# Experts' weights as plain fp32 on two 64-column halves of the PE array, unsplit, with contiguous stationary operands and 16 raw weight buffers

## The chip, the core and the metric

The kernel runs on one core of one Trainium2 chip. The metric is the device time of one execution in microseconds; of several executions the median counts. One execution was also recorded by the hardware profiler, and all rows below come from that record. The engines are called PE (matrix products; PEld is its load of the stationary operand), DVE (vector), ACT (scalar functions), POOL (GpSimd) and SP (the queue that starts most transfers).

## The reference, cut to what matters

Two model blocks follow each other on 256 tokens of width 1024. The change touches only the end of the second one, a mixture of 32 experts in four groups. Every token goes to two experts of one group; an expert is a gated unit of width 512.

```
def _hier_moe(h, rt_g, rt_g_b, rt_e, rt_e_b, ex_gate, ex_up, ex_down):
...
    top_val, top_idx = lax.top_k(le_grp, TOP_K_IN_GROUP)
    wts = jax.nn.softmax(top_val, axis=-1) * p_top
    e_flat = (grp[:, None] * E_PER_GROUP + top_idx.astype(jnp.int32)).reshape(-1)
...
    def expert_block(args):
        idx, w, e = args
        xb = tok_pad[idx]
        hb = jax.nn.silu(xb @ ex_gate[e]) * (xb @ ex_up[e])
        return (hb @ ex_down[e]) * w[:, None]
```

All is float32. The weights of one expert are three matrices of 2 MB each.

## The kernel before, in words

The program is written with a scheduler that orders the instructions of each engine by priority and readiness and places the semaphores. Products that need more than one pass of PE's fast fp32r format are made from an exact pair of parts: a high part (ACT casts the fp32 tile to fp32r, line 141) and a lower part (DVE subtracts it from the fp32 tile, line 142).

The last stage is `Block2.moe` (line 2265). `route` (line 1906) finds each token's experts, normalises and modulates the tokens (lines 1947 to 1950) and splits them into the parts `tok` (`xh`, `xl`). The pairs of token and expert are laid out in slots of 64 rows, one or more for each expert. 29 slots are always worked on (`SURE`); code for up to 39 stands behind a branch. The experts of the first `FIXED` slots are known without routing, so their weights can be fetched early (`fetch`, line 2095).

`slots` (line 2225) runs a software pipeline over the slots. For slot j:

- `gather` (line 2125), for slot 0 alone and then for four slots at once, multiplies one-hot masks with the tokens' parts: 32 products with the token columns as stationary operand, taken with a stride of 8 elements. It gives X, with 64 columns of high and 64 of low parts for each of 8 row blocks.
- `slot_up` (line 2148) fetches gate and up weights in four pieces of 1 MB. Each is cast and subtracted into parts (`split_w`, line 161). For each row block there is one product of X (128 stationary columns: high and low together) with the weights' high part, and one of X's 64 high columns with the weights' lower part. They collect in one bank of PSUM, whose lower 64 rows hold what the low parts of X give.
- `slot_hidden` (line 2169) transposes by a product with `both`, which adds the two row halves, applies the gate, and splits the result into H. The stationary operand G is read with a stride of four elements.
- `slot_down` (line 2187) does the same as `slot_up` with H and two pieces of the down weights, for the slot before; the result is scaled and split into Y.
- `slot_add` (line 2210) adds Y to the tokens' rows through a one-hot mask that POOL builds, for the slot before that.

Raw weights lie in 8 tiles of 8 KB a partition (`raws(8)`, line 2345), their parts in 6 pairs of half tiles (`parts(3)`). Transfers of weights are issued by SP in order; each waits until its raw tile is free, which is when ACT and DVE have read it. In the routing, splits of the first pieces are held back behind the masks of the first gather (`issue_after(self.placed.ins)`).

One plain fp32 product appears in the trace as two load records and two product records, one fp32r product as one of each.

Of the kernel before, what the change touches and what calls it, by code (L numbers as in the profile page):

```python
# [9 lines left out]
F32R = mybir.dt.float32r  # L10
# [5 lines left out]
P = 128  # L16
# [7 lines left out]
def bc(ap, n):  # L24
    """A last axis of n repeats."""
    return ap.unsqueeze(len(ap.shape)).to_broadcast(list(ap.shape) + [n])
# [6 lines left out]
class Kern:  # L33
# [15 lines left out]
    @contextmanager  # L49
    def const(self, pool):  # L50
        """constants go to this pool"""
        old, self.cp = self.cp, pool
        yield
        self.cp = old

    @contextmanager
    def raws(self, n, **where):
        """n tiles of 8 KB for weights as they come"""
# [6 lines left out]
    def parts(self, n, **where):  # L65
        """n pairs of 8 KB for their parts"""
# [6 lines left out]
    @contextmanager  # L73
    def banks(self, **n):
        """how many banks of PSUM each tag has"""
# [11 lines left out]
    def beside(self, gen, tags, rate=1):  # L87
        """tags: the PSUM tags it uses for those it names; rate: its steps to one of the main sequence's"""
# [59 lines left out]
    def load_w(self, src, a, b):  # L148
        """src: DRAM [128, a, b]; gives its f32r parts, each as a function of the row block."""
# [8 lines left out]
    # the lower parts of one in so many come from GpSimd (of none for 0)  # L158
# [14 lines left out]
    def col(x, k):  # L173
        """column block k of an operand in one tile, or in a tile for each"""
# [7 lines left out]
    def proj_T(self, w, x, evac, tag="acc"):  # L182
        """w: DRAM [K, n*512]; x: (hi, lo) [128, K/128, 256]; evac(m, psum [128, 256]) with m in 128s. In steps."""
# [20 lines left out]
    def proj_N(self, w, x, evac, tag="acc", halves=False):  # L204
        """w: DRAM [K, n*512]; evac(half, c, psum [128 t, 512])."""
# [22 lines left out]
    def rsqrt(self, out, v, eps, shape):  # L228
        """out = (v + eps) ** -0.5 on small tiles."""
# [10 lines left out]
    def vec_load(self, items, name):  # L240
        """items: DRAM vectors of n*128, to rows of a tile"""
# [9 lines left out]
    def vec_done(self, loaded):  # L251
        """[128, total], and the start of each"""
# [7 lines left out]
    def ln_stats(self, x, width, eps, name, both=True, junk=None):  # L260
        """x: [128, width]; gives mean and variance, then rstd and (with both) -mean*rstd. On the scalar engine with
        junk [128, width] (and the sum of squares for the variance)."""
# [23 lines left out]
    def bcast_row(self, out, row):  # L286
        """out [128, n] from a DRAM vector [n]."""
        self.nc.sync.dma_start(out, row.unsqueeze(0).to_broadcast([P, row.shape[0]]))

    def gelu(self, out, ps, shape, sp):  # L290
        """tanh form of gelu, from PSUM or SBUF."""
# [10 lines left out]
class Residual:  # L302
    """x_new = LN(alpha * x_old + mix) * gain + bias, with its transposed parts."""
# [9 lines left out]
    def rows(self, gain_row, bias_row):  # L313
        """loads what affine takes"""
# [2066 lines left out]
```

## Time and profile before

| what | value |
|---|---|
| median of 3 runs | 2226.78 us (2226.62 to 2240.33) |
| profiled execution, span | 2225.8 us |
| PE busy | 2028.0 us (91%) |
| DVE busy | 1774.8 us (80%) |
| ACT busy | 1292.5 us (58%) |
| POOL busy | 427.6 us (19%) |
| read from HBM | 398.46 MB, 180 GB/s over the span |

The span is the time from the first to the last instruction of the recorded execution. The stage of the slots takes the last quarter of it. A busy share is an average over stages with different limits; records of PE overlap, because products are pipelined, so the distance between starts says more than their length.

### The profile page before, as it was taken

What the parts mean: (1) busy time and instruction counts of PE and PEld (TensorE: products, weight loads), DVE (VectorE), ACT (ScalarE), POOL (GpSimd) and SP (SyncE); (2) the same over time, 40 slices, a digit from 0 to 9 for tenths busy, and PEclk for the clock granted to TensorE, in tenths of its full rate; (3) what the DMA queues carried; (4) which work ended last, traced back from release to release, by engine and by line L of the source; (5) the groups of instructions that cost most, each with busy time, mean ns of one, the idle gap of its engine ahead of it and who ended that gap; (6) DMA issues with size and microseconds to landing.
All of it is one profiled execution on the core that took longest, in us unless ns stands there. A gap on an engine that the chain in (4) does not pass through costs nothing. (4 is left out here: it accounts for less than half of the span.)

```text
span 2225.8 us, 36150 instructions
## 1 busy us (share of the span) xinstructions
PE 2028.0 (91%) x13468; PEld 1726.5 (78%) x13468; DVE 1774.8 (80%) x3843; ACT 1292.5 (58%) x2287; POOL 427.6 (19%) x307
## 2 busy tenths in 40 slices
PE   6999988999988989999999799698879999999995
PEld 6878978888877889888888689487668777777764
DVE  7768887684659688776895798979678988889897
ACT  4655555565445655554434464665348778778874
POOL 1211100100003121100001000000043555465442
PEclk9999999999989999989999899799979999999998
DMA  5455445642432444634784330002258988989882
GB/s 178 162 176 188 154 165 182 207 144 84 133 114 95 133 133 152 220 114 133 234 276 151 100 118 35 1 1 98 101 224 308 340 321 328 333 323 331 327 325 102
DMA packets 156162, 403.19 MB, mean 181 GB/s; under 512 B 13054, under 2 KB 61242, under 8 KB 133706
## 3 DMA queue, kind: packets, MB, share of 16 engines
q1 hardware_dynamic: 148714, 396.17, 51.3%
q0 software_dynamic: 1664, 3.04, 0.5%
q10 hardware_dynamic: 5600, 1.59, 0.3%
q8 instruction: 108, 1.77, 0.3%
q14 instruction: 76, 0.62, 0.1%
HBM read 398.46 MB, written 2.31 MB: 180 GB/s over the span
## 5 line engine op out<-in xcount | busy, mean ns | idle before, releaser
L142 DVE TENSOR_TENSOR wlo<-raw,whi 128x1024 fp32r<-128x1024 f32 (+1 forms) x650 | 794.6, 1254 | 120.9 <-ACT whi L141 115.2
L141 ACT CAST whi<-raw 128x1024 fp32r<-128x1024 f32 x680 | 689.4, 1048 | 309.2 <-PE acc L113 150.7
L113 PE MATMUL mm<-xTh_m,whi 128*128 128x256 f32 x704 | 204.7, 291 | 0.5 <-DVE modT L124 0.3
L113 PE MATMUL mm<-xTh_m,wlo 128*128 128x256 f32 x704 | 201.7, 287 | 1.7 <-DVE wlo L142 1.7
L113 PE MATMUL mm<-xTl_m,whi 128*128 128x256 f32 x704 | 202.3, 287 | 0.0
L113 PE MATMUL mm<-wlo,m_X 128*64 128x512 f32 x464 | 180.6, 409 | 10.2 <-DVE wlo L142 8.7
L113 PE MATMUL mm<-whi,m_X 128*128 128x512 f32 x464 | 182.0, 401 | 0.1
L142 POOL TENSOR_TENSOR wlo<-raw,whi 128x1024 fp32r<-128x1024 f32 x30 | 94.9, 3164 | 445.1 <-ACT whi L141 434.5
L2122 POOL TENSOR_SCALAR m_ot<-posb,m_r 128x256 fp32r<-128x256 f32 x29 | 98.1, 3384 | 261.4 <-PE acc L113 261.3
L113 PEld LDWEIGHTS mm<-xTh_m,whi 128*128 128x128 f32 x704 | 134.9, 192 | 5.6 <-issue 2.3
L113 PEld LDWEIGHTS mm<-xTh_m,wlo 128*128 128x128 f32 x704 | 135.5, 192 | 4.2 <-DVE wlo L142 2.8
L113 PEld LDWEIGHTS mm<-xTl_m,whi 128*128 128x128 f32 x704 | 134.9, 192 | 2.2 <-issue 0.7
L113 PEld LDWEIGHTS mm<-both,m_G 128*128 128x128 f32 x464 | 115.4, 323 | 5.7 <-ACT m_G L2165 0.4
L113 PEld LDWEIGHTS mm<-whi,m_X 128*128 128x128 f32 x464 | 88.6, 191 | 28.1 <-ACT whi L141 1.2
L113 PEld LDWEIGHTS mm<-wlo,m_X 128*64 128x64 f32 x464 | 62.0, 138 | 58.7 <-DVE wlo L142 47.0
L113 PE MATMUL mm<-both,m_G 128*128 128x64 f32 x464 | 107.3, 363 | 0.0
L113 PE MATMUL acc<-xTh_f,whi 128*128 128x256 f32 x320 | 94.1, 295 | 5.4 <-DVE gl_sq L124 5.4
L113 PE MATMUL acc<-xTh_f,wlo 128*128 128x256 f32 x320 | 93.3, 292 | 2.7 <-DVE wlo L142 2.7
L113 PE MATMUL acc<-xTl_f,whi 128*128 128x256 f32 x320 | 93.3, 292 | 0.6 <-DVE xTl_f L142 0.6
L113 PE MATMUL acc<-xTh_in,whi 128*128 128x256 f32 x320 | 93.2, 292 | 0.5 <-ACT whi L141 0.4
L113 PE MATMUL acc<-xTh_in,wlo 128*128 128x256 f32 x320 | 92.3, 290 | 0.8 <-DVE wlo L142 0.8
L113 PE MATMUL acc<-xTl_in,whi 128*128 128x256 f32 x320 | 92.0, 288 | 0.0
(911 smaller groups left out, 5444.5 us busy)
## 6 DMA issues: line engine op xcount, KB each, us to landing
raw<-in_w_in_dram SPq DMA_DIRECT2D x70, 1024.0 KB
raw<-in_ffn_w_dram SPq DMA_DIRECT2D x66, 1024.0 KB
raw<-in_ex_gate_dram SPq DMA_DIRECT2D x58, 1024.0 KB
raw<-in_ex_up_dram SPq DMA_DIRECT2D x58, 1024.0 KB
raw<-in_ex_down_dram SPq DMA_DIRECT2D x58, 1024.0 KB
raw<-in_w_ada_dram SPq DMA_DIRECT2D x24, 1024.0 KB
raw<-in_w_out_dram SPq DMA_DIRECT2D x12, 1024.0 KB
raw<-in_w_branch_c_dram SPq DMA_DIRECT2D x4, 1024.0 KB
```

Of the source, the lines that this page charges most:

```text
L113: self.nc.tensor.matmul(out, lhsT, rhs, start=start, stop=stop)
L141: first = self.nc.scalar.copy(hi, src)
L142: (e or self.nc.vector).tensor_tensor(out=lo, in0=src, in1=f32(hi), op=ALU.subtract)
L2122: e.tensor_scalar(out=out, in0=a[1], scalar1=b[1], scalar2=None, op0=ALU.is_equal)
```

## The change: what it does

- Weights are no longer split. `next_w` gives the raw fp32 tile, and gate, up and down are plain fp32 products straight from it.
- X holds 64 fp32 columns for each row block (the gather now adds the tokens' high and low parts in PSUM), and H is plain fp32. A product thus has 64 stationary columns. Row blocks alternate between the lower and the upper 64 rows of the PSUM bank; `both` in `slot_hidden`, and the mask of `slot_add`, add the halves, as they did before.
- Stationary operands are contiguous: the tokens are written permuted (`xk`) before they are split, G is taken in blocks of 128 columns, and the down weights' rows are read in matching order, in pieces of 2 x 4 KB a partition where they were 8 KB.
- 16 raw tiles take the place of 8, and the parts' pool goes. Three slots have a fixed expert, where there were two. The holding back behind `placed` and `split_h` goes.
- In `slots`, a step of a gather that goes on beside a slot is one of four with eight products each, where it was two of eight with four.

```
-    FIXED, SURE, MID, SLOTS = 2, 29, 32, 39
+    FIXED, SURE, MID, SLOTS = 3, 29, 32, 39
...
+            xk = self.t_(pool, "r_xk", [P, 2, D], tag="r_xT")
             for h in range(2):
                 kk.stt(xn[:, h], x[:, h], mv[h][:, 0:1], s2, ALU.subtract, ALU.mult)
-                kk.stt(xn[:, h], xn[:, h], rs[h][:, 0:1], h2, ALU.mult, ALU.add)
-                kk.split(self.xh[:, h], self.xl[:, h], xn[:, h])
+                kk.stt(xk[:, h].rearrange("t (k p) -> t p k", k=KD), xn[:, h].rearrange("t (p k) -> t p k", k=KD),
+                       rs[h][:, 0:1], h2.rearrange("t (p k) -> t p k", k=KD), ALU.mult, ALU.add)
+                kk.split(self.xh[:, h], self.xl[:, h], xk[:, h])
...
-        w = a["ex_down_2"][0][e].rearrange("o (p k) d -> p (o k) d", k=4)
+        w = a["ex_down_2"][0][e].rearrange("o (k p) d -> p (o k) d", k=4)
...
-        c = [list(self.chunks(j)) for j in range(2)]
-        order = c[0][:4] + c[1][:4] + c[0][4:]
-        self.ahead = [(kk.raw_w(*w), w[1], w[2]) for w in order[:kk.RAW]]
+        c = [list(self.chunks(j)) for j in range(self.FIXED)]
+        order = c[0][:4]
+        for i in range(1, self.FIXED):
+            order += c[i][:4] + c[i - 1][4:]
+        self.ahead = [kk.raw_w(*w) for w in order[:kk.RAW]]
...
         if not self.ahead:
-            return kk.load_w(*w)
-        raw, a, b = self.ahead.pop(0)
+            return kk.raw_w(*w)
+        raw = self.ahead.pop(0)
         if self.later:
-            n = self.later.pop(0)
-            self.ahead.append((kk.raw_w(*n), n[1], n[2]))
-        if not self.ahead:
-            return kk.split_w(raw, a, b)
-        with kk.tc.issue_after(self.placed.ins):
-            return kk.split_w(raw, a, b)
+            self.ahead.append(kk.raw_w(*self.later.pop(0)))
+        return raw
...
-        X = self.t_(sp, f"m_X{n}", [P, KD, n, 2, 64], F32R, bufs=min(n, 2))
-        for k in range(KD):
-            ps = kk.psum(tag="bg" if n > 1 or k % 2 else "mm")
-            for i, xp in enumerate((self.xh, self.xl)):
+        X = self.t_(sp, f"m_X{n}", [P, KD, n, 64], bufs=min(n, 2))
+        for kp in range(KD // 2):
+            ps = kk.psum(tag="bg" if n > 1 or kp % 2 else "mm")
+            for i in range(2):
                 for h in range(2):
-                    xv = xp[:, h].rearrange("t (p k) -> t k p", k=KD)
-                    kk.mm(ps[:, i * T:(i + 1) * T], xv[:, k], oh[:, h], start=h == 0, stop=h == 1)
-            pv = ps.rearrange("p (i s r) -> p s i r", i=2, s=4)
-            self.last = kk.nc.scalar.copy(X[:, k], pv[:, 0:n])
+                    for part in (self.xh, self.xl):
+                        xv = part[:, h].rearrange("t (k p) -> t k p", k=KD)
+                        kk.mm(ps[:, i * T:(i + 1) * T], xv[:, 2 * kp + i], oh[:, h], start=h == 0 and part is self.xh,
+                              stop=h == 1 and part is self.xl)
+            pv = ps.rearrange("p (i s r) -> p i s r", i=2, s=4)
+            self.last = kk.nc.scalar.copy(X[:, 2 * kp:2 * kp + 2], pv[:, :, 0:n])
...
-                hi, lo = self.next_w(next(w))
+                raw = self.next_w(next(w))
                 for k in range(4):
-                    d = 4 * q + k
-                    xb = X[:, d].rearrange("p i r -> p (i r)")
-                    if d < KD - 1:
-                        kk.mm(ps, xb, hi(k), start=d == 0, stop=False)
-                    kk.mm(ps[0:64], X[:, d, 0], lo(k), start=False, stop=False)
-                    if d == KD - 1:
-                        kk.mm(ps, xb, hi(k), start=False, stop=True)
+                    d, o = 4 * q + k, ps[64 * (k % 2):64 * (k % 2) + 64]
+                    kk.mm(o, X[:, d], raw[:, k], start=d < 2, stop=d >= KD - 2)
...
-            gv = G[:, n].rearrange("s (p k) -> s k p", k=4)
             for k in range(4):
-                kk.mm(g[:, n, k], gv[:, k], self.both)
+                kk.mm(g[:, n, k], G[:, n, k * P:(k + 1) * P], self.both)
...
-        kk.stt(h, h, 0.5, g[:, 1], ALU.mult, ALU.mult)
-        H = t("m_H", [P, 4, 2, 64], F32R, bufs=2)
-        self.split_h = kk.split(H[:, :, 0], H[:, :, 1], h)
+        H = t("m_H", [P, 4, 64], bufs=2)
+        kk.stt(H, h, 0.5, g[:, 1], ALU.mult, ALU.mult)
...
-            hi, lo = self.next_w(next(w))
+            raw = self.next_w(next(w))
             for c in range(2):
...
+                    kk.mm(ps[c][64 * k:64 * k + 64], H[:, 2 * q + k], raw[:, k, c * 512:(c + 1) * 512], start=q == 0,
+                          stop=q == 1)
...
-            for i, _ in enumerate(more):
-                if i == 1 and j + 1 < nxt:
+            for _ in more:
+                if j + 1 < nxt:
                     break
...
-    with kk.raws(8), kk.parts(3), kk.banks(acc=4, mm=4):
+    with kk.raws(16), kk.banks(acc=4, mm=4):
```

## Rows read from the trace of the kernel before

**Rows 1.** Windows: each engine's busy time (and instructions) in stretches of time.

```profile
core 0: us, PE busy (x) PEld busy (x) DVE busy (x) ACT busy (x) POOL busy (x), PEclk, DMA share, GB/s
1612.00:1616.00 4.00, 1.73 (x13) 1.11 (x11) 3.85 (x6) 3.69 (x5) 0.00 (x0) 1.00 1.00 424
1728.00:1732.00 4.00, 4.00 (x19) 3.25 (x20) 4.00 (x5) 3.11 (x5) 4.00 (x3) 1.00 1.01 397
1900.00:2100.00 200.00, 195.34 (x833) 147.51 (x832) 177.02 (x177) 159.07 (x207) 100.50 (x53) 1.00 0.89 328
```

**Rows 2.** Waits from 1550 us (SP's from 1500): total us, times, longest.

```profile
PEld mm L113 <- DVE wlo L142: 47.9, 105, 1.1
...
SPq L155 <- DVE wlo L142: 494.0, 168, 30.8
```

**Rows 3.** Groups of instructions by form from 1550 us: busy us, mean ns | idle before.

```profile
L142 DVE TENSOR_TENSOR wlo<-raw,whi 128x1024 fp32r<-128x1024 f32 x356 | 438.4, 1284 | 22.8 <-ACT whi L141 20.9
L141 ACT CAST whi<-raw 128x1024 fp32r<-128x1024 f32 x356 | 353.3, 1051 | 19.5 <-PE acc L113 9.4 <-DMA raw<-in_ex_gate_dram 5.4 <-PE mm L113 4.2
L113 PE MATMUL mm<-whi,m_X 128*128 128x512 f32 x464 | 182.0, 401 | 0.1
...
L113 PEld LDWEIGHTS mm<-both,m_G 128*128 128x128 f32 x464 | 115.4, 323 | 5.7 <-ACT m_G L2165 0.4
...
L113 PE MATMUL mm<-m_oh,tok 128*128 128x256 f32 x256 | 65.9, 369 | 2.4 <-DVE m_oh L2123 2.4
L113 PEld LDWEIGHTS mm<-wlo,m_X 128*64 128x64 f32 x464 | 62.0, 138 | 58.7 <-DVE wlo L142 47.0
```

**Rows 4.** Timeline of PE in one steady slot: start us, us, what.

```profile
1900.30 1.85 PE L113 MATMUL mm<-both,m_G 128*128 128x64 f32 x8
...
1902.23 0.40 PE L113 MATMUL mm<-whi,m_H 128*128 128x512 f32 x1
1902.47 0.39 PE L113 MATMUL mm<-wlo,m_H 128*64 128x512 f32 x1
...
1919.52 1.85 PE L113 MATMUL mm<-both,m_G 128*128 128x64 f32 x8
```

**Rows 5.** Timeline of PE and PEld, plain fp32 products on 32-column strips (line 1058).

```profile
79.20 1.92 PE L113 MATMUL bg<-raw,ada_cs 128*32 128x512 f32 x8 [2.83 <-DVE ada_cs L1048]
...
79.66 0.12 PEld L113 LDWEIGHTS bg<-raw,ada_cs 128*32 128x32 f32 x2 [0.31 <-issue]
80.09 0.12 PEld L113 LDWEIGHTS bg<-raw,ada_cs 128*32 128x32 f32 x2 [0.30 <-issue]
81.05 0.19 PEld L113 LDWEIGHTS acc<-whi,xTh_in 128*128 128x128 f32 x1 [0.84 <-issue]
```

**Rows 6.** Timeline of PE, products with contiguous stationary operands.

```profile
733.66 0.28 PE L113 MATMUL acc<-xTl_f,whi 128*128 128x256 f32 x1
733.78 0.28 PE L113 MATMUL acc<-xTh_f,wlo 128*128 128x256 f32 x1
...
1565.25 1.30 PE L113 MATMUL mm<-r_rt,modT 128*128 128x36 f32 x10
```

**Rows 7.** Timeline of SP's queue, transfers of the first experts' weights.

```profile
1554.90 36.22 SPq L155 DMA_DIRECT2D raw<-in_ex_gate_dram  x2
...
1609.53 1.16 SPq L155 DMA_DIRECT2D raw<-in_ex_up_dram  x2
```

**Rows 8.** Timeline of PE, the first slot, hidden of slots 1 and 28, last down.

```profile
1630.38 7.95 PE L113 MATMUL mm<-m_oh,tok 128*128 128x256 f32 x32 [2.44 <-DVE m_oh L2123]
...
1640.37 0.47 PE L113 MATMUL mm<-whi,m_X 128*128 128x512 f32 x1
...
1675.69 0.68 PE L113 MATMUL mm<-both,m_G 128*128 128x64 f32 x3
...
2189.03 1.85 PE L113 MATMUL mm<-both,m_G 128*128 128x64 f32 x8
...
2198.36 0.40 PE L113 MATMUL mm<-whi,m_H 128*128 128x512 f32 x1
```

More of the change, by code (lines that the diff above doesn't have):

```diff
@@ L2097, in fetch @@
         kk = self.kk
-        assert self.FIXED == 2
-        c = [list(self.chunks(j)) for j in range(2)]
-        order = c[0][:4] + c[1][:4] + c[0][4:]
-        self.ahead = [(kk.raw_w(*w), w[1], w[2]) for w in order[:kk.RAW]]
+        c = [list(self.chunks(j)) for j in range(self.FIXED)]
+        order = c[0][:4]
+        for i in range(1, self.FIXED):
+            order += c[i][:4] + c[i - 1][4:]
+        assert kk.RAW <= len(order)
+        self.ahead = [kk.raw_w(*w) for w in order[:kk.RAW]]
         self.later = order[kk.RAW:]
@@ L2133, in gather @@
         for h in range(2):
-            self.placed = self.either(e, oh[:, h], (self.io, self.io), (at[:, 2 * h:2 * h + 1], at[:, 2 * h + 1:2 * h + 2]))
-        X = self.t_(sp, f"m_X{n}", [P, KD, n, 2, 64], F32R, bufs=min(n, 2))
-        for k in range(KD):
-            ps = kk.psum(tag="bg" if n > 1 or k % 2 else "mm")
-            for i, xp in enumerate((self.xh, self.xl)):
-                for h in range(2):
-                    xv = xp[:, h].rearrange("t (p k) -> t k p", k=KD)
-                    kk.mm(ps[:, i * T:(i + 1) * T], xv[:, k], oh[:, h], start=h == 0, stop=h == 1)
-            pv = ps.rearrange("p (i s r) -> p s i r", i=2, s=4)
-            self.last = kk.nc.scalar.copy(X[:, k], pv[:, 0:n])
+            self.either(e, oh[:, h], (self.io, self.io), (at[:, 2 * h:2 * h + 1], at[:, 2 * h + 1:2 * h + 2]))
+        X = self.t_(sp, f"m_X{n}", [P, KD, n, 64], bufs=min(n, 2))
+        for kp in range(KD // 2):
+            ps = kk.psum(tag="bg" if n > 1 or kp % 2 else "mm")
+            for i in range(2):
+                for h in range(2):
+                    for part in (self.xh, self.xl):
[4 more added lines that the diff above has]
+            self.last = kk.nc.scalar.copy(X[:, 2 * kp:2 * kp + 2], pv[:, :, 0:n])
             yield
@@ L2191, in slot_down @@
         for q in range(2):
-            hi, lo = self.next_w(next(w))
+            raw = self.next_w(next(w))
             for c in range(2):
-                cs = slice(c * 512, (c + 1) * 512)
                 for k in range(2):
-                    f = 2 * q + k
-                    hb = H[:, f].rearrange("p i r -> p (i r)")
-                    if f < 3:
-                        kk.mm(ps[c], hb, hi(k)[:, cs], start=f == 0, stop=False)
-                    kk.mm(ps[c][0:64], H[:, f, 0], lo(k)[:, cs], start=False, stop=False)
-                    if f == 3:
-                        kk.mm(ps[c], hb, hi(k)[:, cs], start=False, stop=True)
+                    kk.mm(ps[c][64 * k:64 * k + 64], H[:, 2 * q + k], raw[:, k, c * 512:(c + 1) * 512], start=q == 0,
+                          stop=q == 1)
         Y = self.t_(mp, "m_Y", [P, 2, D], F32R)
@@ L2205, in slot_down @@
             s = slice(c * 512, (c + 1) * 512)
-            with kk.tc.issue_after(self.split_h.ins):
-                kk.split(Y[:, 0, s], Y[:, 1, s], ps[c], scale=self.wslot[:, j:j + 1])
+            kk.split(Y[:, 0, s], Y[:, 1, s], ps[c], scale=self.wslot[:, j:j + 1])
         return Y
```

## The prediction

> **What bounds the kernel now.** I read the windows first, then the waits, the groups of instructions and the timeline of PE.
>
> The change touches only the last stage, the mixture of experts: 29 slots of 64 token rows, one after the other. From 1900 to 2100 us PE is busy 195.34 of 200 us at a granted clock of 1.00 (the 2.4 GHz level), DVE 177.02, ACT 159.07, and the DMA engines 0.89 of the time at 328 GB/s [rows 1]. So four resources are nearly full at once, and the question is which ends last. PE waits only 47.9 us in all for lower weight parts from DVE, while SP's queue spends 494.0 us waiting for DVE to release a raw weight tile [rows 2]. The transfers are thus late because their buffers are, not the reverse.
>
> How full PE really is must be read from starts, since records overlap: a 512-wide product lasts 0.401 us in its record [rows 3], but the next starts 0.235 us later (1902.23, 1902.47) [rows 4]. Per slot there are 16 + 16 products of gate and up (464/29 each of high and low parts [rows 3]; down has half as many, 8 + 8), and 8 that add a slot's rows to the tokens: 56 x 0.235 = 13.2 us. The transposes into hidden units are 464/29 = 16 records [rows 3], eight of which take 1.85 us; less the tail of the last, (1.85 - 0.40)/7 = 0.207 each, so 3.3 us [rows 4]. The gather has 256 records, 32 of them for slot 0, so 224/28 = 8 a slot [rows 3], at (7.95 - 0.41)/31 = 0.243: 1.9 us [rows 8]. Sum 18.4 us. One slot's period is 1919.52 - 1900.30 = 19.2 us [rows 4], and over the 27 from the second to the last it is (2189.03 - 1675.69)/27 = 19.01 [rows 8]. PE is the bound, with about 0.8 us a slot lost in waits; DVE (12 x 1.284 = 15.4 us a slot for lower parts alone [rows 3]) is close behind.
>
> **The change, part by part.**
>
> *Splits.* 12 casts of 1.05 us on ACT and 12 subtractions of 1.28 on DVE a slot go away [rows 3]. Neither engine is the bound, so this gives nothing by itself except part of PE's 0.8 us; what it does is make PE the releaser of the raw tiles.
>
> *Products.* 48 records at one pass become 24 plain fp32 products with 64 stationary columns, alternating between the two halves of the output partitions. The trace has this shape once, in the modulation (line 1058): four plain fp32 products of 512 columns, two on one 32-column strip and two on another. They appear as 8 records (two per product) and all 8 fit into 1.92 us, the last included; weight loads come two at a time, at 79.66 and 80.09, so two records start together every 0.43 us [rows 5]. One product alone is then two steps, 0.86 us, and two on different strips share those steps: 0.43 us a product. The strips there are 32 wide and here 64; I take the same. Per slot 24 x 0.43 = 10.3 us instead of 48 x 0.235 = 11.3. The gain here is small; the bounds are 0.43 (full overlap) and 0.86 (none).
>
> The loads at 79.66 and 80.09 run while products are still streaming [rows 5]. The rule in the Trainium skill that speaks most against this change is in "TensorE: Matmul & The Clock Gate", Part 3: a weight load overlaps a running product only where the row groups differ, and here both halves use all 128 rows. The trace does not agree with it; by it the sum would be the third rival's.
>
> A change of shape costs something: the last pair at 79.2 us starts at 80.09 + 0.43 = 80.52, streams to 80.95, and the next full-width load starts at 81.05 [rows 5]. So 0.1 us a change; a slot has 7 or 8 changes (gate, add, up, add, gather, down, hidden): 0.75 us. The Trainium skill says the same in kind ("TensorEngine Tiling (Array Packing)", Key Properties: changing the tiling mode drains the engine), without a figure.
>
> *Contiguous stationary operands.* Hidden: the loads of a stationary operand read with a stride of four elements take 0.323 us [rows 3]; ten plain fp32 records with a contiguous operand take 1.30 us, (1.30 - 0.28)/9 = 0.113 each [rows 6]. 16 x 0.113 = 1.8 us instead of 3.3. Gather: as many records as before (the parts are now summed in PSUM); 256-wide products with a contiguous operand start 0.11 us apart [rows 6]: 8 x 0.113 = 0.9 us instead of 1.9. The token parts must be written permuted (line 1949, two passes of 1.28 us like [rows 3]); the cost lies between nothing and a doubling, 2.6 us; I take nothing, because the pass reads and writes as many elements.
>
> *Sum on PE per slot.* 10.3 + 1.9 (adding) + 1.8 + 0.9 = 14.9 us; with 0.75 for changes and the 0.8 of waits seen now, 16.4 us. This is 2.6 below 19.01; over 27 periods 70.5 us.
>
> *The front.* The first gather's 32 records shrink by 0.13 us each: slot 0 starts at 1640.37 - 4.2 = 1636.2 [rows 8]. Then gate and up 6.9, the gather for four slots 3.6, hidden 1.8, gate and up of slot 1 6.9, down of slot 0 3.4, changes 0.5: hidden of slot 1 starts at 1659.3 instead of 1675.69 [rows 8], 16.4 us earlier.
>
> *The tail.* From the last hidden (2189.03) to the last down (2198.36) are 9.3 us [rows 8]: there H is split and queues behind weight splits. After: 1.8 for the transposes and, estimated from 1.28 us for 1024 columns, about 1.5 for a tanh and two DVE passes of 256, with semaphores 3.7. That gives 5.6 us. The final normalisation stays.
>
> *Buffers and transfers, what is late next.* Eight tiles of 8 KB and the parts give way to 16 tiles. Now the first pieces go out at 1554.90 and the last of the eight at about 1610 [rows 7]. With 16, about 13 follow from 1608 without a pause, and by 1642 all are there. After that the queue only follows PE, up to 16 pieces ahead. 174 pieces of 1.049 MB are needed, 171 of them from 1608. The rate is bounded by 424 GB/s (PE nearly idle), 397 (all engines busy) and 328/0.89 = 369 (the steady stretch, if its gaps were filled) [rows 1]. At 369 the last piece lands at 1608 + 179.3/0.369 = 2094, and some 27 us of down, scaling, adding and normalisation follow: 2121. The sum below ends later, so PE remains the bound, by a thin margin. A slot at 16.4 us asks for 384 GB/s in the long run, which only the 16 pieces of lead make possible at 369.
>
> *The third fixed expert* changes only when pieces of slot 2 may start, and the code for more slots is reached only above 29; the routing of the reference's inputs gives 28 experts with pairs (that of slot 2 among them) and one second slot, 29 both ways. GpSimd's masks (100.50 us in 200, about 9.7 a slot [rows 1]) fit below 16.4 and stay hidden.
>
> Total: 2225.8 - 70.5 - 16.4 - 5.6 = 2133.3 us of span. The profiled span is 1.0 us under the median of 2226.78, so 2134 us.
>
> **The rivals.**
>
> First, the transfers set the pace as they do now: two streams of raw fp32 into PE might disturb the DMA writes as the splits do. For it: with all engines busy the rate was once 397 but 328 over the long stretch [rows 1]. Against it: SP was then waiting for DVE [rows 2], and the rate was 424 with few readers [rows 1]. At 328 GB/s the last piece lands at 1608 + 179.3/0.328 = 2155, and the time is 2183. The same region is reached if the scheduler cuts the alternation so that halves run alone: three such places a slot cost 3 x 0.43 us, 35 us in all, 2169.
>
> Second, slower than before: the two halves do not run together. Then a product costs 0.86 us, 29 x 24 x 0.43 = 299 us more: 2433. It turns to a loss from (2226.8 - 2134)/696 = 0.133 us above 0.43, so from 0.56 us a product. Against it stand the 8 records in 1.92 us [rows 5]; for it, that those were 32-wide strips and four products only.
>
> Third, the loads of the stationary halves are not hidden. A 64-column load takes 0.138 us [rows 3]; one before each of a half's 24 records adds 3.3 us a slot, 96 in all: 2230, no change. (The rule of the Trainium skill's "TensorE: Matmul & The Clock Gate", Part 3, leads here.)
>
> Fourth, better than forecast: the waits of now were the splits' and the changes cost nothing. 14.9 us a slot, 27 x 1.5 = 40 us less: 2094, if the transfers reach 397 GB/s (1608 + 452 + 27 = 2087).
>
> **How the numbers follow.** Forecast case, 2115 to 2155: 0.52. Transfers or broken pairs, 2155 to 2185: 0.20. Better, 2090 to 2115: 0.15. Loads exposed, about 2230: 0.05. No overlap, far slower: 0.08. The range 2095 to 2185 leaves out the last two and the edge of the fourth. About 1% is what a measurement of this kernel can tell from no change. Faster by more than 1%: 0.87; within 1%: 0.05, the third rival; slower: 0.08, the second.
>
> **What would show it.** Right: in the stage of the slots, records of 512 columns starting in pairs 0.43 us apart; hidden records 0.11 apart; a period near 16.4 us; the hidden units of slot 1 near 1659; DVE and ACT below a quarter busy; SP waiting for PE, and DMA at 370 GB/s or more. Wrong: single records 0.43 apart (second rival), pairs 0.57 apart (third), or PE waiting for raw tiles from DMA with the queue always full (first). The prediction falls most easily on the rate of the transfers, and on what a change of shape costs PE.

## The result, and the profile after

| | median (us) | range | ratio to before, 95% interval |
|---|---|---|---|
| before | 2229.51 | 2226.62 to 2240.33 | |
| after | 2129.99 | 2128.09 to 2130.41 | 0.9542 [0.9515, 0.9568] |

The forecast was 2134 us, 2095 to 2185. The span of the profiled execution fell from 2225.8 to 2128.3 us, by 97.5. The windows of after, over stretches like those of [rows 1]:

```profile
core 0: us, PE busy (x) PEld busy (x) DVE busy (x) ACT busy (x) POOL busy (x), PEclk, DMA share, GB/s
1612.00:1616.00 4.00, 4.00 (x25) 3.24 (x23) 3.09 (x16) 1.50 (x4) 0.00 (x0) 0.67 1.01 428
1900.00:2050.00 150.00, 149.80 (x742) 67.88 (x740) 21.11 (x36) 32.26 (x55) 38.20 (x53) 1.00 0.98 390
```

In the steady stretch DVE fell from 177.02 of 200 us to 21.11 of 150 and ACT from 159.07 of 200 to 32.26 of 150. PE has no gap left, and the transfers went from 328 to 390 GB/s at a share of 0.98. From these columns alone one cannot tell whether PE or the transfers set the pace; that was the main question for the experiments. One steady slot on PE (the timeline: start us, us, what), beside [rows 4]:

```profile
1899.56 5.37 PE L113 MATMUL mm<-raw,m_X 128*64 128x512 f32 x24
1904.86 1.20 PE L113 MATMUL mm<-m_oh,tok 128*128 128x256 f32 x8
1905.99 1.94 PE L113 MATMUL mm<-raw,m_X 128*64 128x512 f32 x8
1907.76 1.89 PE L113 MATMUL mm<-raw,m_H 128*64 128x512 f32 x8
1909.58 2.00 PE L113 MATMUL mm<-both,m_G 128*128 128x64 f32 x16
1911.50 1.94 PE L113 MATMUL mm<-raw,m_H 128*64 128x512 f32 x8
1913.46 2.35 PE L113 MATMUL acc<-m_Y,m_ot 128*128 128x512 f32 x8
1915.75 5.37 PE L113 MATMUL mm<-raw,m_X 128*64 128x512 f32 x24
```

A slot takes 1915.75 - 1899.56 = 16.19 us. Products with 64 stationary columns on one half of the output rows are half-width work here, those with 128 full-width. PE goes over from one to the other six times in a slot: before and after the gather's 8 records, the 16 of the hidden units and the 8 of adding. The loads of the stationary halves come two at a time, 0.43 us apart, while products run (timeline of PEld):

```profile
1900.04 0.14 PEld L113 LDWEIGHTS mm<-raw,m_X 128*64 128x64 f32 x2 [0.29 <-issue]
1900.47 0.14 PEld L113 LDWEIGHTS mm<-raw,m_X 128*64 128x64 f32 x2 [0.29 <-issue]
```

The groups of instructions that answer [rows 3] (busy us, mean ns | idle before):

```profile
L113 PE MATMUL mm<-raw,m_X 128*64 128x512 f32 x928 | 211.9, 598 | 0.0
L113 PEld LDWEIGHTS mm<-both,m_G 128*128 128x128 f32 x464 | 54.1, 191 | 23.5 <-issue 21.1 <-ACT m_Y L133 2.4
L113 PE MATMUL mm<-m_oh,tok 128*128 128x256 f32 x256 | 38.1, 297 | 2.4 <-DVE m_oh L2124 2.4
L2123 POOL TENSOR_SCALAR m_ot<-posb,m_r 128x256 fp32r<-128x256 f32 x29 | 26.8, 924 | 318.6 <-PE acc L113 318.5
L124 DVE SCALAR_TENSOR_TENSOR r_xk<-r_xn,rs_moe,r_h 128x1024 f32<-128x1024 f32 x2 | 3.9, 1976 | 0.4 <-PE mm L113 0.4
```

The contiguous loads of the hidden units take 191 ns where they took 323. SP now waits for PE where it waited for DVE's splits [rows 2]:

```profile
SPq L155 <- PE mm L113: 320.8, 156, 12.5
```

First gather, first slot, hidden units of slots 1 and 28, last down (timeline of PE, beside [rows 8]):

```profile
1635.51 5.37 PE L113 MATMUL mm<-m_oh,tok 128*128 128x256 f32 x32 [2.44 <-DVE m_oh L2124]
...
1644.68 7.08 PE L113 MATMUL mm<-raw,m_X 128*64 128x512 f32 x30
...
1669.13 2.00 PE L113 MATMUL mm<-both,m_G 128*128 128x64 f32 x16
...
2098.79 2.00 PE L113 MATMUL mm<-both,m_G 128*128 128x64 f32 x16
...
2104.97 3.65 PE L113 MATMUL mm<-raw,m_H 128*64 128x512 f32 x16
```

The 97.5 us are: 1675.69 - 1669.13 = 6.6 in front of the hidden units of slot 1; 27 periods of (2098.79 - 1669.13)/27 = 15.91 us instead of 19.01, 83.7 in all; and 36.7 - 29.5 = 7.2 from the start of the last hidden units to the end of the span.

Where the 3.1 us a slot come from shows when, over these 27 periods, the distances from each record's start to the next on PE are added up by kind (a wait counts to the group ahead of it). Gate, up and down take 10.75 us a slot (12.33 before), hidden units 1.93 (3.08), the gather 0.96 (1.43), adding 2.27 (2.17). So half of the gain, 1.6 us, stands at the two contiguous operands and half at the products with their waits.

### The profile page after: what moved, and what is told of

It reads as the page before. It is cut to its first block, busy times and chain, and to the rows that moved or that the text cites. A ratio compares the mean times of both kernels' runs of the same rounds, so it can differ in the third digit from the quotient of the medians.

```text
span 2128.3 us, 34994 instructions
## 1 busy us (share of the span) xinstructions
PE 1947.1 (91%) x13468; PEld 1527.1 (72%) x13468; DVE 1346.7 (63%) x3466; ACT 945.9 (44%) x1878; POOL 260.8 (12%) x307
## 5 line engine op out<-in xcount | busy, mean ns | idle before, releaser
L141 ACT CAST whi<-raw 128x1024 fp32r<-128x1024 f32 (+1 forms) x332 | 345.0, 1047 | 299.8 <-PE acc L113 147.7
L142 DVE TENSOR_TENSOR wlo<-raw,whi 128x1024 fp32r<-128x1024 f32 (+1 forms) x302 | 366.4, 1218 | 100.2 <-ACT whi L141 97.0
L124 DVE SCALAR_TENSOR_TENSOR m_h<-m_h,mm 128x256 f32<-128x256 f32 x29 | 12.2, 422 | 328.7 <-ACT m_h L133 328.7
L113 PE MATMUL mm<-raw,m_X 128*64 128x512 f32 x928 | 211.9, 598 | 0.0
L113 PEld LDWEIGHTS mm<-raw,m_X 128*64 128x64 f32 x928 | 62.1, 136 | 115.4 <-issue 112.3
L2163 ACT COPY m_G<-mm 128x512 f32<-128x512 f32 x58 | 34.0, 586 | 201.7 <-PE mm L113 201.7
L113 PE MATMUL mm<-raw,m_H 128*64 128x512 f32 x464 | 110.2, 599 | 0.0
L124 DVE SCALAR_TENSOR_TENSOR m_Y<-mm,wslot,m_Y 128x512 fp32r<-128x512 f32 x58 | 43.6, 751 | 67.6 <-ACT m_Y L133 64.5
L113 PEld LDWEIGHTS mm<-both,m_G 128*128 128x128 f32 x464 | 54.1, 191 | 23.5 <-issue 21.1
```

Of the source, the lines that this page charges most:

```text
L113: self.nc.tensor.matmul(out, lhsT, rhs, start=start, stop=stop)
L124: return self.nc.vector.scalar_tensor_tensor(out=out, in0=a, scalar=s, in1=b, op0=op0, op1=op1)
L141: first = self.nc.scalar.copy(hi, src)
L142: (e or self.nc.vector).tensor_tensor(out=lo, in0=src, in1=f32(hi), op=ALU.subtract)
L2163: kk.nc.scalar.copy(G[:, n], ps)
```

## The experiments

Every ratio is to the kernel before, run on the same chip.

| kernel | median (us) | ratio, 95% interval | period of a steady slot (us) |
|---|---|---|---|
| after | 2129.99 | 0.9542 [0.9515, 0.9568] | 16.2 |
| halves in runs of two | 2159.42 | 0.9678 [0.9661, 0.9694] | 17.3 |
| one half only | 2426.39 (one run) | | 26.4 |
| hidden units' operand strided | 2204.89 | 0.9881 [0.9865, 0.9898] | 18.2 and 19.4 |
| gather's operand strided | 2158.38 | 0.9672 [0.9654, 0.9690] | 17.2 |
| before, contiguous operands alone | 2182.88 | 0.9783 [0.9765, 0.9801] | 17.9, some 18.8 |
| 8 raw tiles | 2138.22 | 0.9585 [0.9569, 0.9601] | 16.55 |
| less work on PE | 2072.97 (one run) | | 12.4, then 14.8 |
| fixed order | 2109.45 | 0.9452 [0.9431, 0.9472] | 15.2 |
| fixed order, 8 raw tiles | 2110.74 | 0.9467 [0.9440, 0.9494] | 15.2 |
| fixed order, strided read | 2108.97 | 0.9455 [0.9432, 0.9478] | 15.2 |
| token passes on POOL | 2135.32 | 0.9582 [0.9566, 0.9598] | 16.2 |

### Do the halves share their time?

```
-                for k in range(4):
+                for k in (0, 2, 1, 3):
...
-            for c in range(2):
-                for k in range(2):
+            for k in range(2):
+                for c in range(2):
```

> The changed kernel, but the products come in runs of two on the same half of the output partitions (halves 0, 0, 1, 1) instead of in turns; same products, same sums. My theory, that a product is two passes of 0.43 us and that a pass runs beside another only if its neighbour in the order of issue stands on the other half: in a run of four products two passes find no partner, so four products take 6 passes, 2.58 us, instead of 4, 1.72 us. That is 0.215 us more a product, 5.2 us a slot of 24, about 150 us in all: 2280 us, period 21.4 us. The rival that the halves do not work at the same time at all, and 0.43 us is simply what a product with 64 columns takes: no change, 2130 to 2140 us. The rival that PE looks ahead and pairs what fits: the same, no change.

Not my theory: 29 us more, not 150. The products still ran in pairs (four of them, 8 records, in 1.94 us as in after), so if the halves do share their time, PE finds the partner of a product although the next one in the program's order stands on the same half. (The records do not name the half of a product; its order is taken from the program.) The 1.1 us a slot come from elsewhere. With the two output banks of a down ending together, PE waits for the scaled outputs, and adding is cut in two by products (two more changes of shape):

```profile
1909.98 1.45 PE L113 MATMUL acc<-m_Y,m_ot 128*128 128x512 f32 x5 [0.87 <-ACT m_Y L133]
1911.36 1.94 PE L113 MATMUL mm<-raw,m_X 128*64 128x512 f32 x8
1913.23 0.96 PE L113 MATMUL acc<-m_Y,m_ot 128*128 128x512 f32 x3
```

That left open whether the halves matter at all. The next run put everything on one of them:

```
-                    d, o = 4 * q + k, ps[64 * (k % 2):64 * (k % 2) + 64]
-                    kk.mm(o, X[:, d], raw[:, k], start=d < 2, stop=d >= KD - 2)
...
+                    d, o = 4 * q + k, ps[0:64]
+                    kk.mm(o, X[:, d], raw[:, k], start=d == 0, stop=d == KD - 1)
...
-                kk.mm(g[:, n, k], G[:, n, k * P:(k + 1) * P], self.both)
+                kk.mm(g[:, n, k], G[0:64, n, k * P:(k + 1) * P], kk.ident[0:64, 0:64])
```

> The changed kernel with all of a slot's products on one half of the output partitions (64 rows through the whole slot; the sum over the two halves falls away). The run with the halves in runs of two still ran in pairs 0.43 us apart, so PE either picks a partner a few records ahead, or the halves have nothing to do with it and 0.43 us is what such a product takes. This tells the two apart. Theory of the halves: a product alone takes two passes of 0.43 us, 0.86 us; 24 x 0.43 more, 10.3 us a slot, 29 slots: about 2430 us, period 26.5 us. The rival that a product with 64 columns takes 0.43 us by itself: 2125 to 2135 us.

2426 us, and the loads come singly, 0.43 us apart (timeline of PEld):

```profile
1900.08 0.14 PEld L113 LDWEIGHTS mm<-raw,m_X 128*64 128x64 f32 x1 [0.29 <-issue]
1900.51 0.14 PEld L113 LDWEIGHTS mm<-raw,m_X 128*64 128x64 f32 x1 [0.29 <-issue]
```

So a product of 64 stationary and 512 moving columns is two passes of 0.43 us, and the two halves take theirs at the same time. This is worth 2426 - 2130 = 296 us; the second rival of the prediction had 299 for its absence.

### What are the contiguous operands worth?

```
-        w = a["ex_down_2"][0][e].rearrange("o (k p) d -> p (o k) d", k=4)
+        w = a["ex_down_2"][0][e].rearrange("o (p k) d -> p (o k) d", k=4)
...
-                kk.mm(g[:, n, k], G[:, n, k * P:(k + 1) * P], self.both)
+                kk.mm(g[:, n, k], G[:, n].rearrange("s (p k) -> s k p", k=4)[:, k], self.both)
```

> The changed kernel, but the stationary operands of the products that transpose the hidden units are read with a stride of four elements again, as before the change (and the rows of the down weights come in the order that fits). My theory, that contiguity is worth what the loads of before showed: 16 records at 0.207 us instead of 0.113, 1.5 us a slot on PE, which is the bound, 43 us over the slots: 2173 us, period 17.7 us. The rival that these loads are hidden now or that PE is not the bound (transfers are): less than 10 us, 2130 to 2140 us.

75 us more, not 43. The block itself takes 3.95 us instead of 2.00, 1.95 more (1.5 expected), 57 us over 29 slots. The rest is mainly PE's clock. In a part of the slots the down products behind the block take 3.45 us instead of 1.94 (timeline of PE):

```profile
1912.19 3.95 PE L113 MATMUL mm<-both,m_G 128*128 128x64 f32 x16
1916.07 3.45 PE L113 MATMUL mm<-raw,m_H 128*64 128x512 f32 x8
```

and the windows show the granted clock there, in this slot and in the next (PEclk is the third figure from the end):

```profile
1912.20:1916.00 3.80, 3.80 (x18) 3.80 (x16) 0.00 (x0) 0.00 (x0) 0.00 (x0) 1.00 1.03 435
1918.00:1919.50 1.50, 1.50 (x5) 0.06 (x1) 0.75 (x1) 0.54 (x1) 0.00 (x0) 0.50 0.79 333
...
1936.00:1938.00 2.00, 1.98 (x10) 0.58 (x6) 1.35 (x3) 1.19 (x3) 0.00 (x0) 1.00 1.01 426
```

0.50 is the 1.2 GHz level. Before it fell PE had spent 3.95 us on narrow products (64 moving columns) with strided loads. Slots of 18.2 and of about 19.4 us follow each other.

The gather's operand, undone alone:

```
-            xk = self.t_(pool, "r_xk", [P, 2, D], tag="r_xT")
...
-                kk.stt(xk[:, h].rearrange("t (k p) -> t p k", k=KD), xn[:, h].rearrange("t (p k) -> t p k", k=KD),
-                       rs[h][:, 0:1], h2.rearrange("t (p k) -> t p k", k=KD), ALU.mult, ALU.add)
-                kk.split(self.xh[:, h], self.xl[:, h], xk[:, h])
+                kk.stt(xn[:, h], xn[:, h], rs[h][:, 0:1], h2, ALU.mult, ALU.add)
+                kk.split(self.xh[:, h], self.xl[:, h], xn[:, h])
...
-                        xv = part[:, h].rearrange("t (k p) -> t k p", k=KD)
+                        xv = part[:, h].rearrange("t (p k) -> t k p", k=KD)
```

> The changed kernel with the other contiguous operand undone: the tokens are written unpermuted again (one contiguous pass in place) and the gather reads its stationary operands with a stride of eight elements, as before the change. PE's order of work stays the same as in the changed kernel. My theory, that each strided load costs what it cost before the change: 8 records a slot at 0.243 us instead of 0.118, 1.0 us a slot, 28 us over the slots, and 4 us in the first gather, less 1.4 us of the permuted passes: 2130 + 30 = 2160 us, period 17.2 us. The rival seen with the strided hidden units, that PE's granted clock falls behind such a block as well: a further 1 us in a part of the slots, 2170 us or more. The rival that the loads are hidden here: 2128 to 2135 us.

As expected: 2158 us, and the period grew by 1.0 us, just by the longer step (1.20 us in after). The clock stayed at 1.00 from 1900 to 2050 us.

```profile
1912.46 2.19 PE L113 MATMUL mm<-m_oh,tok 128*128 128x256 f32 x8
```

Contiguity alone, in the kernel before (splits, 8 tiles and 128-column products kept; the edits to `chunks`, `gather`, `slot_hidden` and the token write as in the change):

> The kernel before, with its splits into high and low parts, its 48 products a slot and its 8 raw tiles, but with the contiguous stationary operands of the change (hidden units and gather, and the permuted token write). My theory: PE falls from 18.4 to 15.9 us a slot; DVE, busy for 177.02 of 200 us at 19.0 us a slot, that is 16.8 us a slot, is next. The period lands between 16.9 and 17.6 us: 2225.8 - 27 x 1.75 = 2179 us, 2168 to 2192. The rival that the splits already set the pace as much as PE, through the release of the raw tiles: period 18.3 or more, 2205 to 2230 us. The rival that contiguity was the whole gain: period near 16.2, 2150 us.

2183 us: 2.2 of the change's 4.6% come without unsplitting anything. Then DVE is as full as PE, and PE's loads wait for it twice as long as in the kernel before (1700 to 2100 us; this run first, then the kernel before):

```profile
1900.00:2050.00 150.00, 143.08 (x660) 95.67 (x661) 142.53 (x144) 128.49 (x168) 82.30 (x46) 1.00 0.95 349
...
PEld mm L113 <- DVE wlo L142: 62.4, 143, 1.3
PEld mm L113 <- DVE wlo L142: 30.2, 72, 1.1
```

Undone in the changed kernel the two operands cost PE 1.95 + 1.0 us a slot; put into the kernel before they bring only about 1.4. Most of the difference lies in the kernel before itself. There the scheduler scatters the narrow records among 512-wide products, and a strided load runs while a wide product streams. This gather record of the slot of [rows 4] delays the next product by only 0.12 us:

```profile
1916.20 0.29 PE L113 MATMUL mm<-m_oh,tok 128*128 128x256 f32 x1
1916.32 0.40 PE L113 MATMUL mm<-whi,m_X 128*128 128x512 f32 x1
```

By the distances between starts, hidden units and gather take 3.08 + 1.43 us a slot in the kernel before and 1.52 + 1.23 in this run, 1.8 less; the products with the splits take 0.4 of it back (12.71 us a slot instead of 12.33). No run leaves out the splits alone, with both operands strided. If the 75 and the 28 us of the two runs above add, it would take about 2233 us (an estimate), no less than the kernel before; by it, neither part of the change gives the 100 us by itself.

### PE or the transfers?

```
-            if j in (j0, nxt - 4) and nxt < j1:
+            if j == j0 and nxt < j1:
...
-                G, w[j] = self.slot_up(j, mp, self.X.pop(j), lambda n: next(adds, None))
+                G, w[j] = self.slot_up(j, mp, self.X[j if j <= 4 else 1 + (j - 1) % 4], lambda n: next(adds, None))
```

(and adding only where `j - 2` is the first or the last slot)

> The changed kernel with work left out on PE, so that the transfers can be seen by themselves: tokens are gathered for slots 0 to 4 only and these are multiplied again with the later experts' weights, and the outputs of the first and the last slot only are added to the tokens. All products with weights, all hidden units and all transfers stay. PE then has 24 x 0.43 + 1.8 + four changes of shape of 0.17, 12.8 us a slot. My theory, that the engines of the DMA can do 424 GB/s and have slack in the changed kernel: 174 pieces from 1602 us land by 1602 + 182.5 MB / 0.424 = 2032, and some 27 us follow: 2060 us; the period is near 13 while the lead of 16 pieces lasts and 14.8 us after it, with PE waiting for raw tiles. The rival that 390 GB/s is all that the DMA can do beside these products, so that transfers bind the changed kernel as much as PE does: 1602 + 468 + 27, about 2097 us, and the period comes back to 16.1 us. If PE is all that matters: 1669 + 27 x 12.8 + 27, about 2042 us.

My theory held: 12.4 us a slot while the lead of pieces lasts, to 1806 us, then 14.7 to 15.7. In the second part PE waits for raw tiles, and the transfers run at 424 GB/s from 1668 us on:

```profile
1750.00:1800.00 50.00, 50.00 (x261) 21.02 (x258) 9.38 (x16) 11.72 (x20) 0.00 (x0) 1.00 1.01 424
...
1900.00:2000.00 100.00, 88.20 (x430) 33.75 (x429) 14.07 (x24) 18.75 (x32) 0.00 (x0) 1.00 1.02 424
...
1902.35 1.94 PE L113 MATMUL mm<-raw,m_X 128*64 128x512 f32 x8 [0.59 <-DMA raw<-in_ex_up_dram]
```

So the transfers' own floor is 14.8 us a slot, and in the changed kernel a share of 0.98 at 390 GB/s is a queue that follows PE. (My 2060 us was 13 too low, mainly because I let the queue run on without a pause. It nearly stands still from the time when all 16 tiles are full until slot 0 releases some: 51 GB/s from 1643 to 1650 us and 316 from there to 1668, which together lose some 11 us at 424.)

With 8 raw tiles, `kk.raws(8)`:

> The changed kernel with 8 raw tiles instead of 16. My theory after the result: PE is the bound in the steady stretch and the transfers follow it, because the DMA engines can do 424 GB/s, 14.8 us a slot, where PE takes 16.2; 8 tiles, more than a slot's six, are enough. A few us at the front, where fewer pieces are there when the first slot begins: 2130 to 2142 us, period 16.2 to 16.4 us. The rival from the prediction, that a slot of 16.2 us asks for more than the long-run rate of 369 GB/s and that only the 16 pieces of lead make it possible: 6.29 MB / 0.369 = 17.0 us a slot, 2150 us or more, and PE waits for raw tiles from DMA.

The time is in my range, but the period of 16.55 us is neither theory's. PE still has no gap; its order came out another, with adding cut in two:

```profile
1914.60 1.88 PE L113 MATMUL acc<-m_Y,m_ot 128*128 128x512 f32 x6
1916.41 1.94 PE L113 MATMUL mm<-raw,m_X 128*64 128x512 f32 x8
1918.28 0.73 PE L113 MATMUL acc<-m_Y,m_ot 128*128 128x512 f32 x2
```

Two changes of shape more, 0.35 us more: this is a price for a change, 0.17 us, and not one for buffers.

### The price of a change of shape, and a faster version

`mm` keeps the last product it issued, and each group is issued behind it: gate and up; down; adding; a step of the gather; hidden units.

```
+    def behind(self):
+        return self.tc.issue_after(self.pe.ins)
...
             if up:
-                G, w[j] = self.slot_up(j, mp, self.X.pop(j), lambda n: next(adds, None))
...
+                with kk.behind():
+                    G, w[j] = self.slot_up(j, mp, self.X.pop(j), lambda n: None)
+            if down:
+                with kk.behind():
+                    Y[j - 1] = self.slot_down(j - 1, mp, H.pop(j - 1), w.pop(j - 1))
+            with kk.behind():
+                list(adds)
```

> The changed kernel with the order of PE's work in a slot fixed: gate and up, down of the slot before, then all full-width work in one piece (adding, one step of the gather, transposing the hidden units). PE changes between half-width and full-width work twice a slot instead of six times (eight in the first slots). My theory, that a change of shape costs about 0.17 us on PE and PE is the bound: 4 changes less, 0.7 us a slot, 27 x 0.7 = 19 us: 2111 us, period 15.5 us with a gather step and 14.5 without. The rival that transfers at 390 GB/s are the bound of the slots: no change, 2128 to 2132 us. The rival that the fixed order brings a new wait (hidden units or scaled outputs late) of 0.5 us or more a slot: 2125 us or more, and PE idle at that place.

It is faster than both kernels, 2109 us, its interval clear of that of after. The period is 15.2 us with a gather step and 14.2 without:

```profile
1901.78 7.09 PE L113 MATMUL mm<-raw,m_X 128*64 128x512 f32 x32
1908.70 3.60 PE L113 MATMUL mm<-raw,m_H 128*64 128x512 f32 x16
1912.23 2.12 PE L113 MATMUL acc<-m_Y,m_ot 128*128 128x512 f32 x8
1914.19 1.10 PE L113 MATMUL mm<-m_oh,tok 128*128 128x256 f32 x8
1915.13 1.90 PE L113 MATMUL mm<-both,m_G 128*128 128x64 f32 x16
1916.95 1.51 PE L113 MATMUL mm<-raw,m_X 128*64 128x512 f32 x6
```

Of the 1.0 us, 0.33 is adding, which takes 1.96 us from its start to the next group's where it took 2.29: in after its loads wait for DVE's part of the scaled outputs (10.7 us in 25 slots), here they do not. The other 0.67 is put down to the four changes, 0.17 us each, as in the run with 8 tiles. One of the four is adding's own way back to half-width work, and how its 0.33 divides between that and the wait is not shown, so 0.17 is a mean that can be somewhat low. The transfers went along, at 417 GB/s from 1900 to 2050 us. With PE's order alone changed, this also confirms that PE was the bound of after.

The same with 8 raw tiles:

> The kernel with the fixed order of PE's work (2 changes of shape a slot), with 8 raw tiles instead of 16. In the run with 8 tiles before, PE's order came out another, with two changes of shape more a slot, so that run mixed two things; here the order is the same whatever the tiles. At 15.2 us a slot the transfers need 414 GB/s of the 424 that the DMA engines did alone. My theory, that PE is the bound and 8 tiles cover the 4.6 us of a slot in which PE releases none: period 15.2 to 15.3 us, 2106 to 2114 us. The rival that near the full rate the lead of 16 pieces is needed, since what a pause loses is hardly caught up: PE waits for raw tiles from DMA, period 15.5 us or more, 2118 us or more.

2110.74 against 2109.45 us, and the same period: with the order held, the second eight tiles bring nothing that can be measured.

```profile
1900.00:2050.00 150.00, 150.00 (x786) 74.78 (x784) 22.51 (x40) 31.99 (x58) 33.83 (x47) 1.00 1.01 414
```

### The front

```
-                kk.stt(xk[:, h].rearrange("t (k p) -> t p k", k=KD), xn[:, h].rearrange("t (p k) -> t p k", k=KD),
-                       rs[h][:, 0:1], h2.rearrange("t (p k) -> t p k", k=KD), ALU.mult, ALU.add)
-                kk.split(self.xh[:, h], self.xl[:, h], xk[:, h])
+                nc.gpsimd.tensor_scalar(out=xn[:, h], in0=xn[:, h], scalar1=rs[h][:, 0:1], scalar2=None, op0=ALU.mult)
+                nc.gpsimd.tensor_tensor(out=xk[:, h].rearrange("t (k p) -> t p k", k=KD), ..., op=ALU.add)
+                kk.split(self.xh[:, h], self.xl[:, h], xk[:, h], e=nc.gpsimd)
```

> The changed kernel with four of the six passes that prepare the tokens moved from DVE to GpSimd: the scaling with the permuted write (as two passes there) and the low parts. DVE is busy 28.66 of 35 us from 1605 to 1640. My theory, that DVE's queue sets the start of the first gather: DVE is rid of 2 x (1.98 + 1.21) us and of the wait for the logits' products ahead of them, so the gather starts some 6 us sooner, near 1629.5 instead of 1635.51, if GpSimd's six passes of about 3 to 4 us each, from 1614 on, are done by then: 2124 us. The rival that GpSimd becomes the late one (its passes take longer while DVE works beside them): the gather starts at 1637 or later, no gain or a loss of up to 10 us, 2130 to 2140 us.

By the medians a loss of 5 us, the intervals just touching. The gather starts at 1636.12 us, in an execution whose routing began 3.9 us earlier than that of after (the tokens' transposes at 1602.93 instead of 1606.80); counted from there it starts 4.5 us later. The time is the rival's, but the reason is neither theory's. POOL was done in time, at 1626. It was DVE that stood still. While POOL's passes ran, DVE's smallest products took as long as a pass (timeline):

```profile
1616.70 4.68 POOL L1952 TENSOR_TENSOR r_xk<-r_xn,r_h 128x1024 f32<-128x1024 f32 x2
...
1616.81 2.27 DVE L121 TENSOR_TENSOR r_o<-io,r_grp 128x8 f32<-128x8 f32 x1
1619.11 2.29 DVE L121 TENSOR_TENSOR r_l<-r_lg,r_o 128x16 f32<-128x16 f32 x1
...
1626.25 0.18 DVE L121 TENSOR_TENSOR r_l<-r_l,r_l8t 128x16 f32<-128x16 f32 x1
```

Last, on the kernel with the fixed order, the token pass turned round, and the first slot not held:

```
-                kk.stt(xk[:, h].rearrange("t (k p) -> t p k", k=KD), xn[:, h].rearrange("t (p k) -> t p k", k=KD),
-                       rs[h][:, 0:1], h2.rearrange("t (p k) -> t p k", k=KD), ALU.mult, ALU.add)
+                kk.stt(xk[:, h].rearrange("t (k p) -> t k p", k=KD), xn[:, h].rearrange("t (p k) -> t k p", k=KD),
+                       rs[h][:, 0:1], h2.rearrange("t (p k) -> t k p", k=KD), ALU.mult, ALU.add)
```

> The kernel with the fixed order, with two changes at the front: the tokens' permuted pass walks in the order of its output (contiguous write of 512 bytes, reads with a stride of eight elements) instead of in the order of its input (write with a stride of 512 bytes, 1.97 us where the unpermuted pass took 1.28), and the first slot's products are not held behind the pairs' weights (they began at 1646.47 in the run with the fixed order and at 1643.04 to 1644.68 in the changed kernel). My theory: a strided read costs DVE less than a strided write, 1.3 to 1.6 us a pass, 0.8 to 1.3 us sooner, and 2 us from the first slot: 2105 to 2107 us, pass and start to be read in the trace. The rival that the stride costs the same on either side: 1.97 us a pass again, 2107 to 2109 us. The rival that two strided reads cost more than one strided write: over 2.2 us a pass, 2108 to 2112 us.

The first rival: the stride costs as much on the reads, 2.05 us a pass, and the median does not move. The first slot did come sooner: from the start of the gather to its first product 7.8 us instead of 9.9. In this execution 1.7 of these 2 us went again in the last down products, 5.35 us instead of 3.65 (granted clock 0.76 from 2083 to 2088 us, where the fixed order had 1.00); whether they are worth anything is not shown.

```profile
L128 DVE SCALAR_TENSOR_TENSOR r_xk<-r_xn,rs_moe,r_h x2: 2052/2054/2056, 1619.9 to 1622.1; 128x1024 f32<-128x1024 f32 x2
```

## Why the prediction held, step by step

**Products: right.** 0.43 us each on two halves, as [rows 5] had it for strips of 32 columns. The run on one half shows the 0.86. The second and third rivals are out (pairs 0.43 us apart, where the third wanted 0.57). The rule of the Trainium skill weighed in the prediction ("TensorE: Matmul & The Clock Gate", Part 3) is not borne out: two 64-column loads a step of 0.43 us run beside products on the same 128 rows, and the step is no longer than the 0.43 us of a single load and product on one half.

**Contiguous operands: right for the changed kernel, wrong for what they replaced.** With contiguous loads the 16 records of the hidden units take 1.9 us (1.8 forecast) and the 8 of the gather 1.1 (0.9), a change of shape included. But the prices of before were taken from blocks: 3.3 us from [rows 4] and 1.9 from [rows 8], where the slots spent 3.08 and 1.43 on average (1.66 for the gather where a step of it stands beside the slot) on records scattered among wide products. So the gain was 1.15 + 0.47 us a slot, not 1.5 + 1.0. Of this only the 0.8 of waits, which is what these prices left of the period of before, entered the forecast; the rest of it is added up from the changed kernel's own terms. For a whole strided block the price from [rows 4] was too low instead: the first record's load stands ahead of the start I counted from. The strided run has 3.95 us for 16 records, (3.95 - 0.40)/15 = 0.237 each, not 0.207, and the clock on top.

**Changes of shape and waits: the sum right, its parts not quite.** Six changes of about 0.17 us and 0.33 us in adding, 1.3 us, where 0.75 and 0.8 stood. I read 0.1 us from one way out of a half-width block [rows 5] and took it for every change, and I counted 7 or 8 of them. (The 47.9 us of [rows 2] are waits of PE's loads; the products of gate and up themselves stood idle 8.7 us for DVE's parts.) The fourth rival (no such cost) is out.

**Period: 16.2 against 16.4.** The sum of 14.9 for PE's work stood: the fixed order with its two changes gives 14.9 + 2 x 0.17 = 15.2. The mean over 27 periods, 15.9, is lower mainly because the last four slots have no gather step beside them (14.9 us each) and I charged it to all; 83.7 us instead of 70.5.

**Front: wrong, 6.6 us instead of 16.4.** Four things are missing. The routing begins 2.7 us later, which the change does not do: 1.6 of it came near 1515 us, where the granted clock was 0.67 in this execution and 1.00 in that of before. (Executions differ there by several us: that of the fixed order with 8 tiles is 6.9 ahead of after at 1600 us.) The permuted write, which I took as free, costs 1976 instead of 1278 ns, twice, and starts later: 2.4 us in all from the end of the residual to the first gather. That gather gives 2.6 us and not 4.2, at a clock of 0.74 from 1636 to 1641 us. And from slot 0's first product (1643.04) to the hidden units of slot 1 it takes 26.1 us, not 23.1: I left out the gather step of slot 1 (1.2) and the products for the pairs' weights in between (about 1.2).

**Tail: 7.2 us against 5.6, for other reasons in part.** From the last hidden units to the last down 9.3 us became 6.2, not 3.7: a half of the down before and adding stand in between, 1.96 + 2.29 us, which I left out. Behind it I had put nothing. There the last down's products take 1.25 us less without the splits, and 2.6 us come where I did not look, at the branch over the code for more slots (start us, us, what; before, then after):

```profile
2213.59 1.28 DVE L271 BATCH_NORM_STATS2 st_fin<-x 128x6 f32<-128x512 f32 x2 [2.92 <-DVEq L2280]
2116.24 1.29 DVE L271 BATCH_NORM_STATS2 st_fin<-x 128x6 f32<-128x512 f32 x2 [0.28 <-DVEq L2269]
```

DVE stands idle there for 2.92 us (3.00 in the run with contiguous operands alone) and for 0.28 in every run without splits. Why is not shown.

**Transfers: PE is the bound, but not by a thin margin.** The step that failed is the rate: 369 GB/s as a long-run bound, from a stretch in which the queue was held up by buffers [rows 1, 2]. Not held up they do 424, a floor of 14.8 us a slot (and at the front 418 from 1602 to 1643 us, by when all 16 pieces were there, as forecast). So the lead of 16 pieces is not what makes the pace possible; 8 tiles do as well even at 15.2 us. The first rival is out.

In sum the front fell short by 9.8 us, and the slots and the tail gave 13.2 and 1.6 more. That the forecast of 2134 us came within 4 of the measured time is luck in so far as these errors, and those inside the period, cancel; products, bound and period near 16.4 us were right. The third fixed expert was not undone in any run.

## What to carry to other kernels

Where PE and DVE are both nearly full, a change that frees only one of them can give less than its own price: contiguous operands alone gave 2.2 of 4.6% here. Take the price of a strided load from the place where it stands; in a block of its own it costs more than between wide products. When narrow and full-width products alternate, put all full-width work of a period into one piece; the scheduler's own order cost 20 us. A transfer share near 1.00 is no sign that transfers bind; leave work out on the other side and see whether the rate moves.

## What the runs showed of the hardware

- PE runs products of two column halves together (0.43 us a product, 0.86 on one half), and still does, 8 records in 1.94 us, when the program puts two of the same half behind each other.
- A stationary operand with a stride of four or eight elements costs about 0.24 us a record in a block (0.11 to 0.12 contiguous), but a single one of the gather between wide products only 0.12.
- A block of 3.95 us of narrow products with strided loads was followed by the 1.2 GHz level (0.50) in about half of the slots; the same block with contiguous loads, 2.00 us, and the strided gather of 2.19 us were not, in the steady stretch.
- DVE and POOL shut each other out. A DVE product of 8 columns took 2.27 us during a pass on POOL, 0.17 us otherwise; and POOL's masks, 3384 ns each beside DVE's splits before the change, take 924 ns after it. The Trainium skill states such a lock between the two for whole instructions ("SBUF — State Buffer", SBUF: two separate sides); the trace agrees, with 2.27 us on DVE beside 4.68 us for two passes on POOL.
- Transfers of 1 MB ran at 424 GB/s for 100 us on end while PE streamed at full clock, and 8 pieces of lead were enough at 414.
- A DVE pass over 1024 columns cost 1.98 us with a strided write and 2.05 us with strided reads, 1.28 us with neither.
